# Making the weight sums of a seven-product last projection in another stage, partly by accumulating transfers

## The chip, the cores and the metric

The kernel runs on one core of one Trainium2 chip. The metric is device time in microseconds; the kernel before takes 1702.14 us, the median of three runs from 1701.0 to 1705.25. In the profile PE is TensorE's matmul, PEld its weight load, DVE is VectorE, ACT is ScalarE, POOL is GpSimd and SP is SyncE. SP, ACT and POOL also issue DMA transfers (SPq, ACTq, POOLq), each in its own program order.

## What is computed

The reference is a decoder trunk of two layers. Each layer mixes tokens in three branches and then adds a gated feed-forward with a causal convolution. A final norm ends it. The change touches only the feed-forward of the second layer and what feeds it:

```python
def conv_ffn(h, w_up, conv_w, conv_b, w_down):
    S = h.shape[1]
    u = h @ w_up                                   # 512 x 1024 @ 1024 x 5632
    up = jnp.pad(u, ((0, 0), (CONV_WIDTH - 1, 0), (0, 0)))
    c = conv_b
    for j in range(CONV_WIDTH):
        c = c + conv_w[j] * up[:, j:j + S]
    gate, val = jnp.split(c, 2, axis=-1)
    return (jax.nn.silu(gate) * val) @ w_down      # 512 x 2816 @ 2816 x 1024
...
    for l in range(DEPTH):
...
        x = x + conv_ffn(rmsnorm(x, norm2_g[l]), ffn_w_up[l], ffn_conv_w[l], ffn_conv_b[l], ffn_w_down[l])
    return rmsnorm(x, final_g)
```

## The kernel before

All tensors are float32. A product is made to float32 accuracy from three matmuls (`mm3`, L151): each operand is split into a rounded high part and a low remainder, and high by low, high by high and low by high are summed in PSUM. A weight tile of 128 by 512 (256 KB) is loaded by SP into `wr` (`load`, L121) and split by `part` (L131): ScalarE makes the high part (L139, `wh` or `sh`), VectorE the low one (L140, `wl` or `sl`). `unit` (L99) hands the splits out in the order of a plan that a first pass over the program writes down. It keeps splits a few tiles ahead of the matmuls (`AHEAD`: three in the up projection of a layer, four in the first part of the last projection) and loads three, or there six, tiles ahead of the splits. The framework's scheduler decides the final order of each engine's instructions from their priorities and dependencies. Where the code says `keep_in_program_order` (also as `po`), the order written is kept.

A layer's mixer is followed by the output projection (`wout`), by `ffn_up`, and then by `ffn_down` in layer 0 or by `last` in layer 1.

`ffn_up` makes 44 outputs of 128 by 512 (ff columns by tokens), in the order gate i, value i for i = 0 to 21. Each output is 8 k-tiles times 3 matmuls. VectorE takes it from PSUM (L1082, `fu`), ScalarE and VectorE apply the convolution (L1084 to L1086, `cv`), ScalarE the silu (L1090), and VectorE multiplies (L1091, `fth`). In layer 0 each `fth` is split for `ffn_down`. In layer 1 every second one goes with the one before it, a and b, to `halves` (L1100), which serves `last`. For odd i below 17 `ffn_up` of layer 1 also transposes a tile of x by way of DRAM on POOL's queue (`turned`, L227 to L230, `xT`, `tr` and `xt`).

`last` is the second layer's down projection, the residual and the final norm. It works on pairs of ff chunks, q = 0 to 10, as a product of 2 by 2 blocks by seven block products instead of eight. The weight blocks of pair q are w0 = W[2q] columns 0 to 511, w1 = W[2q] columns 512 to 1023, and w2, w3 the same of W[2q+1]. The activation blocks are the token halves a0, a1 of chunk 2q and b0, b1 of chunk 2q+1. The products 7, 5, 6 and 4 take sums of weight blocks and of activation halves, the products 1, 2 and 3 take w0, w2 and w3 as they are. `last` first runs the products 7, 5, 6, 4 over all q (the last pair in the order 6, 7, 5, 4), 6 matmuls for each weight tile, then product 1 over all q, then 2, then 3. All seven are in PSUM, and the output quarters are put together from them by VectorE (`addx`, `plus`, `post`) with factors of 0.5 or -0.5, the residual in `xt` and the squares for the norm.

The sums of the weight blocks do not depend on x. In the kernel before they are made during layer 0's `ffn_up` (q = 0 to 3) and `ffn_down` (q = 4 to 10), at the places in the table `PRE`. `presum` (L237) loads the four blocks of pair q with POOL's queue into `pre` tiles, and at its next call has VectorE make the four sums in place (L242 to L245) and POOL's queue store them to DRAM as `ts` tiles (L248). In `ffn_up` the tiles come from the 39 tiles of the pool `ff0`, in `ffn_down` from the pool `up`. `last` loads the sums from `ts` as it loads other weights, from the fifth tile on at most ten tiles ahead.

`halves` (L1100) makes for pair q the activation sums `s` and `d` in tiles named `wh` and `wl` by VectorE in operations of 256 columns, and a third sum in place over b's first half. It splits `s` and `b` (two splits of 512 columns: a ScalarE copy and a VectorE subtraction each). POOL's queue stores a0 and b0 as `ab` and d's first half as `s4`, which `last` loads and splits as it goes (`side`, `fetch`, `both`). The final gain `fg` is loaded on POOL's queue after the second pair of `last`.

In the span layer 0's `ffn_up` begins a few us before 511 and its `ffn_down` ends shortly before 866. The second `ffn_up` begins a few us before 1358 and ends at about 1586. `last` runs from there on, with its four summed products up to 1646.

Of the kernel before, what the change touches and what calls it, by code (L numbers as in the profile page):

```python
# [15 lines left out]
L = 2  # L16
# [3 lines left out]
NFF = 22  # L20
# [5 lines left out]
PRE = {(0, "f", 2): 0, (0, "f", 4): 1, (0, "f", 6): 2, (0, "f", 8): 3, (0, "d", 0): 4, (0, "d", 1): 5, (0, "d", 2): 6, (0, "d", 3): 7,  # L26
       (0, "d", 4): 8, (0, "d", 5): 9, (0, "d", 6): 10}
SEQ = "0 H 0 S 0 U S U S 0 S 0 0 S 2 2 Y 0 0 2 1 2 1 2 1 2 1 2 1 2 1 1 1"
NRAW = 3
AHEAD = {None: 2, "p": 4, "r": 3, "f": 3, "u": 5, "q": 4}  # L30
# [21 lines left out]
class Emit:  # L52
    def __init__(self, ctx, tc, a, plan=None):
# [5 lines left out]
        tp = lambda n, b, **k: ctx.enter_context(tc.tile_pool(name=n, bufs=b, **k))  # L59
        self.cp = tp("cp", 1)  # L60
# [60 lines left out]
    def load(self, u):  # L121
        name, l, i, c0, n, _ = u
        raw = self.u(n="wr") if u[5] == "q" and self.nraw % 2 else self.wp.tile([128, 512], F32, name=self.nm("wr"), tag="wr", bufs=NRAW)
        src = self.tsum[i] if name == "tsum" else self.a[name][l, i]
# [112 lines left out]
    def presum(self, l, stage, m):  # L237

        if self.pre:
            q, b = self.pre.pop()  # L240
            V = self.nc.vector
            V.tensor_tensor(b[3], b[3], b[1], op=SUB)  # L242
            V.tensor_tensor(b[1], b[1], b[0], op=SUB)
            V.tensor_tensor(b[0], b[0], b[3], op=ADD)
            V.tensor_tensor(b[2], b[2], b[0], op=SUB)  # L245
            for p, t in zip((7, 5, 6, 4), (b[3], b[1], b[0], b[2])):
                self.tsum[q, p] = self.dp.tile([128, 512], F32, name=self.nm("ts"))
                self.nc.gpsimd.dma_start(self.tsum[q, p], t)  # L248
        q = PRE.get((l, stage, m))
        if q is not None:  # L250
            b = self.fpre.pop(0) if stage == "f" else [self.u(n="pre") for _ in range(4)]
            for i, t in enumerate(b):
                self.nc.gpsimd.dma_start(t, self.a["wdt"][0, 2 * q + i // 2][:, i % 2 * 512:i % 2 * 512 + 512])
            self.pre.append((q, b))
# [69 lines left out]
    def run(self):  # L324
        nc, tc, a, V = self.nc, self.tc, self.a, self.nc.vector
        self.con = self.cp.tile([128, NCC], F32, name="con")
        self.pre, self.tsum = [], {}
# [730 lines left out]
    def ffn_up(self, l, st, x):  # L1058
# [10 lines left out]
        if l == 0:  # L1069
            self.fpre = [[self.f(n="pre") for _ in range(4)] for _ in range(4)]  # L1070
        for i in range(NFF):
            if l == 0 and i % 2 == 0 and 2 <= i <= 10:
                self.presum(l, "f", i)
# [5 lines left out]
            for j in (i, NFF + i):  # L1079
# [7 lines left out]
                cs.append(t)  # L1087
            g, v = cs
# [44 lines left out]
    def last(self, act):  # L1133
# [301 lines left out]
```

## Time and profile before

| | us |
|---|---|
| median of 3 runs | 1702.14 |
| lowest and highest run | 1701.0, 1705.25 |
| the profiled execution's own time | 1701.55 |
| its span | 1699.8 |
| TensorE busy | 1686.0 |
| VectorE busy | 1216.0 |
| ScalarE busy | 800.5 |
| GpSimd busy, DMA issues included | 240.7 |
| mean granted TensorE clock | 0.999 of full speed |

A page of the profile has numbered parts. Part 1 gives the busy time of each engine; a busy TensorE is not one at its peak, since matmuls overlap. The chain that ended last is followed back from the last instruction, at each step to what released it or to the instruction before it on its engine; its pieces in order of time read "start, length, what, how many". A window row gives, for one stretch of time, its length, the busy time of PE, PEld, DVE, ACT and POOL with the number of instructions, the granted clock, the share of the 16 DMA engines in use and the GB/s. A timeline row is "start, duration, engine, line, operation, output<-input, count", with the idle time just before it and what ended it in brackets. A row of a tile's instructions gives the shortest, median and longest duration in ns, then the first and last start.

### The profile page before, as it was taken

How to read it: one execution, taken by the hardware profiler on the slowest of the kernel's cores; microseconds unless marked ns; L12 is line 12 of the kernel's file. 1: busy time of each engine (PE TensorE's matmuls, PEld its weight loads, DVE VectorE, ACT ScalarE, POOL GpSimd, SP SyncE). 2: the span in 40 equal slices, each digit the busy share in tenths (PEclk: the TensorE clock that was granted, in tenths of full speed). 3: DMA queues.
4: the chain of work that ended last, by engine and by line, in shares of the span. 5: the costliest groups of instructions: out<-in, count | busy, mean ns of one | idle time of the engine just before them, and what ended most of it. 6: DMA issues, size and time to landing. Idle time of an engine off the chain costs nothing.

```text
span 1699.8 us, 27851 instructions
## 1 busy us (share of the span) xinstructions
PE 1686.0 (99%) x10214; PEld 1379.6 (81%) x10214; DVE 1216.0 (72%) x2113; ACT 800.5 (47%) x1367; POOL 240.7 (14%) x336
## 2 busy tenths in 40 slices
PE   9999999999999999999999999999999999999998
PEld 7888777788888888888888888778888888888886
DVE  6887746578669877655568888455786698887776
ACT  6563433453345444433346544335542554444565
POOL 2121000003301200003321210000132022110000
PEclk9999999999999999999999999999999999999999
DMA  5236553525544533147743265535254443443775
GB/s 182 87 109 203 174 180 94 174 93 164 190 148 143 196 120 99 63 144 261 247 150 98 91 205 181 179 101 185 88 165 158 155 133 127 134 134 112 242 242 166
DMA packets 147768, 260.01 MB, mean 153 GB/s; under 512 B 19600, under 2 KB 39952, under 8 KB 147632
## 3 DMA queue, kind: packets, MB, share of 16 engines
q1 hardware_dynamic: 122960, 192.87, 36.1%
q0 software_dynamic: 15888, 49.95, 8.9%
q10 hardware_dynamic: 8784, 15.42, 2.5%
q8 instruction: 80, 1.31, 0.3%
q14 instruction: 56, 0.46, 0.1%
HBM read 212.94 MB, written 45.22 MB: 152 GB/s over the span
## 4 chain that ended last, share of the span: by engine, by line
PE 85%; DVE 6%; DMA 5%; issue 2%; ACT 2%; SPq 1%; ACTq 0%; POOL 0%; DVEq 0%; POOLq 0%
PE acc L156 77%; PE sm L664 2%; PE sm L156 2%; DMA wr<-wall 2%; DVE wl L140 2%; PE sm L917 1%; PE sm L571 1%; DMA tr<-bkT 1%; DVE cs L790 1%; DMA wr<-wdt 1%; DVE TMP L788 1%; DMA bkS<-tr 1%; ACT wh L139 1%; DVE sl L140 1%; ACT sh L139 0%
## 5 line engine op out<-in xcount | busy, mean ns | idle before, releaser
L156 PE MATMUL acc<-lo,sh 128*128 128x512 f32 x1108 | 432.3, 391 | 0.2 <-ACT sh L139 0.2
L156 PE MATMUL acc<-hi,sh 128*128 128x512 f32 x1108 | 432.4, 390 | 0.0
L156 PE MATMUL acc<-hi,sl 128*128 128x512 f32 x1108 | 431.0, 390 | 0.2 <-DVE sl L140 0.2
L139 ACT CAST sh<-wr 128x512 fp32r<-128x512 f32 (+1 forms) x375 | 228.8, 616 | 368.6 <-PE acc L156 220.0
L140 DVE TENSOR_TENSOR sl<-wr,sh 128x512 fp32r<-128x512 f32 (+1 forms) x375 | 255.0, 684 | 108.8 <-ACT sh L139 79.3
L140 DVE TENSOR_TENSOR wl<-wr,wh 128x512 fp32r<-128x512 f32 x238 | 168.7, 712 | 144.7 <-ACT wh L139 141.3
L139 ACT CAST wh<-wr 128x512 fp32r<-128x512 f32 x238 | 146.8, 619 | 243.7 <-PE acc L156 139.3
L156 PEld LDWEIGHTS acc<-hi,sl 128*128 128x128 f32 x1108 | 208.1, 188 | 44.4 <-DVE sl L140 0.6
L156 PEld LDWEIGHTS acc<-lo,sh 128*128 128x128 f32 x1108 | 208.1, 188 | 44.3 <-issue 0.9
L156 PEld LDWEIGHTS acc<-hi,sh 128*128 128x128 f32 x1108 | 208.1, 188 | 42.9 <-issue 0.3
L156 PE MATMUL acc<-lo,wh 128*128 128x512 f32 x588 | 232.2, 395 | 1.3 <-ACT wh L139 0.8
L156 PE MATMUL acc<-hi,wl 128*128 128x512 f32 x588 | 230.4, 392 | 1.0 <-DVE wl L140 1.0
L156 PE MATMUL acc<-hi,wh 128*128 128x512 f32 x588 | 229.5, 390 | 0.0
L156 PEld LDWEIGHTS acc<-hi,wl 128*128 128x128 f32 x588 | 110.4, 188 | 26.7 <-DVE wl L140 3.0
L156 PEld LDWEIGHTS acc<-lo,wh 128*128 128x128 f32 x588 | 110.4, 188 | 26.4 <-ACT wh L139 1.6
L156 PEld LDWEIGHTS acc<-hi,wh 128*128 128x128 f32 x588 | 110.5, 188 | 22.1 <-issue 0.2
L156 PE MATMUL acc<-ah,sh 128*128 128x512 f32 x352 | 108.3, 390 | 0.0
L1084 ACT ACTIVATE cv<-fu,pc 128x512 f32<-128x512 f32 x88 | 71.6, 816 | 62.4 <-DVE fu L1082 62.3
L1082 DVE TENSOR_TENSOR fu<-acc,rsF 128x512 f32<-128x512 f32 x88 | 60.6, 688 | 39.1 <-PE acc L156 38.4
L1085 DVE SCALAR_TENSOR_TENSOR cv<-fu,pc,cv 128x511 f32<-128x511 f32 x88 | 65.9, 750 | 29.8 <-ACT cv L1084 29.8
L156 PE MATMUL acc<-wl,hi 128*128 128x512 f32 x212 | 86.2, 407 | 0.0
L156 PE MATMUL acc<-wh,hi 128*128 128x512 f32 x212 | 82.9, 391 | 0.0
(358 smaller groups left out, 2413.4 us busy)
## 6 DMA issues: line engine op xcount, KB each, us to landing
wr<-wall SPq DMA_DIRECT2D x488, 256.0 KB, 2.8
gd<-gth ACTq DMA_DIRECT2D x48, 256.0 KB, 3.2
gth<-gd POOLq DMA_DIRECT2D x48, 256.0 KB, 3.5
pre<-wdt POOLq DMA_DIRECT2D x44, 256.0 KB, 5.6
ts<-pre POOLq DMA_DIRECT2D x44, 256.0 KB, 2.8
wr<-ts SPq DMA_DIRECT2D x44, 256.0 KB, 4.0
wr<-wdn SPq DMA_DIRECT2D x40, 256.0 KB, 4.1
wr<-wdt SPq DMA_DIRECT2D x33, 256.0 KB, 3.7
```

The costliest lines, as they stand in the source:

```text
L139: self.kept(self.nc.scalar.copy(hi[:, :n], raw[:, :n]))
L140: self.kept(self.nc.vector.tensor_tensor(lo[:, :n], raw[:, :n], hi[:, :n], op=SUB))
L156: i = self.nc.tensor.matmul(*x, **y, **kw)
L571: i = T.matmul(pK[hv[1 - h], j, :], bk[hv[h], c, 1, :], x[hv[h], c, :], start=True, stop=True)
L664: po(T.matmul(o, l, r, start=start, stop=True, skip_group_check=True))
L788: V.tensor_tensor(tmp, NS[:, k + 1:, k:k + 1].to_broadcast([128, r, c]), TS[:, k:k + 1, :c].to_broadcast([128, r, c]), op=MUL)
L790: V.tensor_tensor(TS[:, k + 1:, :c], TS[:, k + 1:, :c], tmp, op=ADD)
L917: po(T.matmul(X[h][:, i, :], lhsT, rhs, start=new[h], stop=stop, skip_group_check=True))
L1082: V.tensor_tensor(u, ps, self.rsF, op=MUL)
L1084: A.activation(t, u, AF.Identity, scale=self.p("cw2", j), bias=self.p("cb", j))
L1085: V.scalar_tensor_tensor(t[:, 1:], u[:, :511], self.p("cw1", j), t[:, 1:], op0=MUL, op1=ADD)
```

## The change

The sums move from layer 0 to layer 1's `ffn_up` and the first pairs of `last`. They are made all positive: T7 = w1 + w3, T5 = w0 + w1, T6 = w0 + T7, T4 = w2 + T6. T7 and T5 are made by two transfers each, a load and then a load that adds to the tile (`accum_op`), cut into pieces of 128 elements (512 bytes). T6 and T4 are a load and one VectorE addition each. A generator, `sums`, spreads this over four calls for each pair; it is called once after each output of `ffn_up` (up to i = 20) and once after each of the first six pairs of `last`. Its `pre` tiles have a pool of their own, of six. The scratch space of the software descriptor ring is set to 4096 bytes a partition; the default, which the kernel before has, is 16384. Since the sums have other signs, `halves` makes other activation sums, and `last` subtracts in some places where it added.

In `halves` the two halves of the second split tile, `t`, now come from two different places, d's second half (a0 - a1) and b's second half (b1), and are split by separate instructions of 256 columns. Nothing is written over b any more.

```diff
-PRE = {(0, "f", 2): 0, (0, "f", 4): 1, (0, "f", 6): 2, (0, "f", 8): 3, (0, "d", 0): 4, (0, "d", 1): 5, (0, "d", 2): 6, (0, "d", 3): 7,
-       (0, "d", 4): 8, (0, "d", 5): 9, (0, "d", 6): 10}
+RING = 4096
...
+        self.pp = tp("pp", 6)
...
-        src = self.tsum[i] if name == "tsum" else self.a[name][l, i]
+        src = self.tsum[(l, *i)] if name == "tsum" else self.a[name][l, i]
...
-    def presum(self, l, stage, m):
-
-        if self.pre:
-            q, b = self.pre.pop()
-            V = self.nc.vector
-            V.tensor_tensor(b[3], b[3], b[1], op=SUB)
-            V.tensor_tensor(b[1], b[1], b[0], op=SUB)
-            V.tensor_tensor(b[0], b[0], b[3], op=ADD)
-            V.tensor_tensor(b[2], b[2], b[0], op=SUB)
-            for p, t in zip((7, 5, 6, 4), (b[3], b[1], b[0], b[2])):
-                self.tsum[q, p] = self.dp.tile([128, 512], F32, name=self.nm("ts"))
-                self.nc.gpsimd.dma_start(self.tsum[q, p], t)
-        q = PRE.get((l, stage, m))
-        if q is not None:
-            b = self.fpre.pop(0) if stage == "f" else [self.u(n="pre") for _ in range(4)]
-            for i, t in enumerate(b):
-                self.nc.gpsimd.dma_start(t, self.a["wdt"][0, 2 * q + i // 2][:, i % 2 * 512:i % 2 * 512 + 512])
-            self.pre.append((q, b))
+    def sums(self, l):
+
+        P, V, po, Q, T = self.nc.gpsimd, self.nc.vector, self.tc.keep_in_program_order, NFF // 2, {}
+
+        def get(q, p, n):
+            T[q, p] = self.pp.tile([128, 512], F32, name=self.nm("pre"), tag="pre")
+            add(q, p, n)
+
+        def add(q, p, n, **kw):
+            po(P.dma_start(T[q, p], self.a["wdt"][l - 1, 2 * q + n // 2][:, n % 2 * 512:n % 2 * 512 + 512], **kw))
+
+        def keep(q, *ps):
+            for p in ps:
+                self.tsum[l, q, p] = self.dp.tile([128, 512], F32, name=self.nm("ts"))
+                po(P.dma_start(self.tsum[l, q, p], T.pop((q, p))))
+
+        def both(q, o, i):
+            po(V.tensor_tensor(T[q, o], T[q, o], T[q, i], op=ADD))
+
+        for q in range(Q + 1):
+            if q:
+                both(q - 1, 6, 7)
+                keep(q - 1, 7, 5)
+            if q < Q:
+                get(q, 7, 1)
+                get(q, 5, 0)
+            yield
+            if q:
+                both(q - 1, 4, 6)
+                keep(q - 1, 6, 4)
+            yield
+            if q < Q:
+                add(q, 7, 3, accum_op=ADD, max_dma_last_dim=512)
+                add(q, 5, 1, accum_op=ADD, max_dma_last_dim=512)
+                get(q, 6, 0)
+                get(q, 4, 2)
+            yield
+            yield
+
+    def presum(self, l):
+        if l == L - 1:
+            next(self.sum, None)
...
-        if l == 0:
-            self.fpre = [[self.f(n="pre") for _ in range(4)] for _ in range(4)]
+        self.sum = self.sums(l)
         for i in range(NFF):
-            if l == 0 and i % 2 == 0 and 2 <= i <= 10:
-                self.presum(l, "f", i)
...
                 cs.append(t)
+                if i < 20 or i == 20 and j == i:
+                    self.presum(l)
...
-        V.tensor_tensor(s[:, h[0]], a[:, h[1]], b[:, h[1]], op=ADD)
-        V.tensor_tensor(s[:, h[1]], s[:, h[0]], a[:, h[0]], op=SUB)
-        V.tensor_tensor(d[:, h[0]], b[:, h[0]], s[:, h[1]], op=SUB)
+        V.tensor_tensor(s[:, h[0]], b[:, h[1]], a[:, h[1]], op=SUB)
+        V.tensor_tensor(d[:, h[1]], a[:, h[0]], a[:, h[1]], op=SUB)
+        V.scalar_tensor_tensor(s[:, h[1]], d[:, h[1]], -1.0, b[:, h[1]], op0=MUL, op1=SUB)
+        V.scalar_tensor_tensor(d[:, h[0]], s[:, h[1]], -1.0, b[:, h[0]], op0=MUL, op1=SUB)
         P.dma_start(self.s4[:, h[q % 2]], d[:, h[0]])
-        V.tensor_tensor(b[:, h[0]], a[:, h[0]], a[:, h[1]], op=SUB)
-        return self.split(s, at), self.split(b, at), ab, self.s4
+        t = hi, lo = at(), at()
+        for o, x in ((h[0], d[:, h[1]]), (h[1], b[:, h[1]])):
+            self.nc.scalar.copy(hi[:, o], x)
+            V.tensor_tensor(lo[:, o], x, hi[:, o], op=SUB)
+        return self.split(s, at), t, ab, self.s4
...
-            self.presum(l, "d", m)
...
-                return self.unit("tsum", 0, (q, p), 0)
+                return self.unit("tsum", L - 1, (q, p), 0)
...
+            if q < 6:
+                self.presum(L - 1)
...
-                v[2, q], v[3, q] = addx(pss[5][q], 1, 2 + q), addx(pss[5][q], 1, q)
+                v[2, q], v[3, q] = addx(pss[5][q], 1, 2 + q, -0.5), addx(pss[5][q], 1, q, -0.5)
...
-                V.tensor_tensor(y, y, f0[at - 1], op=ADD)
+                V.tensor_tensor(y, y, f0[at - 1], op=SUB if r else ADD)
...
-                plus(v[3, q], out[1][q], v[3, q])
+                plus(v[3, q], out[1][q], v[3, q], -0.5)
...
-            po(plus(y, out[3][r], y))
+            po(plus(y, out[3][r], y, -0.5))
...
-        nc = _bacc.Bacc("TRN2", target_bir_lowering=False, num_devices=1)
+        nc = _bacc.Bacc("TRN2", target_bir_lowering=False, num_devices=1, dynamic_dma_scratch_size=RING)
```

More of the change, by code (lines that the diff above doesn't have):

```diff
@@ L326, in run @@
         self.con = self.cp.tile([128, NCC], F32, name="con")
-        self.pre, self.tsum = [], {}
+        self.tsum = {}
         self.rst = self.cp.tile([128, 512], F32, name="rst")
@@ L1178, in half, with addx @@
             return t
-        def addx(ps, h, c):
+        def addx(ps, h, c, scale=0.5):
             y = self.r(n="v")
@@ L1185, in addx, with plus @@
                 x = self.xt[4 * h + j][:, c]
-                V.scalar_tensor_tensor(v(y), v(ps), 0.5, x, op0=MUL, op1=ADD)
+                V.scalar_tensor_tensor(v(y), v(ps), scale, x, op0=MUL, op1=ADD)
             return y
-        def plus(y, ps, z):
-            return V.scalar_tensor_tensor(y, ps, 0.5, z, op0=MUL, op1=ADD)
+        def plus(y, ps, z, scale=0.5):
+            return V.scalar_tensor_tensor(y, ps, scale, z, op0=MUL, op1=ADD)
         def square(y, s):
```

## The prediction

> **What bounds the kernel now.** I read the page from the top: busy time, then the chain that ended last, then windows over the stages.
>
> ```profile
> span 1699.8 us, 27851 instructions
> PE 1686.0 (99%) x10214; PEld 1379.6 (81%) x10214; DVE 1216.0 (72%) x2113; ACT 800.5 (47%) x1367; POOL 240.7 (14%) x336
> ```
>
> TensorE is without work for 13.8 us of 1699.8. A busy TensorE need not run at its peak, so the chain of waits gives the pace:
>
> ```profile
> 511.06 355.19 PE acc L156 x1567
> 1358.42 210.36 PE acc L156 x928
> ```
>
> 355.19 / 1567 and 210.36 / 928 are both 0.2267 us for one matmul, and nothing else stands between them. These are layer 0's up and down projections (where the old sums are made) and the second up projection (where the new ones go). The windows agree; columns are us, then busy us of PE, PEld, DVE, ACT, POOL, the clock, the DMA share and GB/s:
>
> ```profile
> 511.00:711.00 200.00, 200.00 (x884) 165.72 (x883) 159.80 (x243) 97.95 (x150) 15.03 (x28) 1.00 0.41 132
> 711.00:866.00 155.00, 155.00 (x685) 128.42 (x685) 87.53 (x140) 51.72 (x88) 34.33 (x64) 1.00 0.61 203
> 1358.40:1568.80 210.40, 210.40 (x930) 174.34 (x929) 173.57 (x280) 97.54 (x152) 35.10 (x64) 1.00 0.40 129
> 1568.80:1573.10 4.30, 3.94 (x16) 2.47 (x14) 4.30 (x8) 3.05 (x6) 0.54 (x1) 1.00 0.14 50
> 1594.00:1612.00 18.00, 18.00 (x80) 14.59 (x79) 13.36 (x22) 11.98 (x22) 0.00 (x0) 1.00 0.94 308
> 1692.60:1699.80 7.20, 0.00 (x0) 0.00 (x0) 1.90 (x5) 2.22 (x7) 0.00 (x0) 0.84 0.34 123
> ```
>
> The tail has 7.2 us of the 13.8, so 6.6 us are idle elsewhere, the start of the kernel included. The built program issues the same TensorE instructions in the same order, but for two neighbours that change places. So the change can win only stalls beside it, and it can lose whatever it makes TensorE wait for.
>
> **What it removes in layer 0.** 44 VectorE operations and 88 transfers of 256 KB on POOL's queue:
>
> ```profile
> L253 POOL DMA_DIRECT2D pre<-wdt x44: 536/538/543, 457.0 to 847.3; - x44
> L248 POOL DMA_DIRECT2D ts<-pre x44: 539/543/548, 539.4 to 857.1; - x44
> L242 DVE TENSOR_TENSOR pre<-pre,pre x11: 683/692/694, 538.4 to 854.0; 128x512 f32<-128x512 f32 x11
> ```
>
> That is 44 x 0.69 = 30 us of VectorE, 88 x 0.54 = 48 us of POOL and 23 MB. TensorE is busy 200.00 of 200.00 and 155.00 of 155.00 us there, so all of it lies behind matmuls: gain 0.
>
> **What it adds in the second up projection.** For each pair of ff chunks (q; 21.76 us, four outputs of 24 matmuls): two loads and two accumulating loads for the tiles 7 and 5, two loads for 6 and 4, two VectorE additions, four stores. Thus eight transfers, as in layer 0, and two VectorE operations in place of four. Layer 0 shows such a load beside an up projection:
>
> ```profile
> 538.00:559.80 21.80, 21.80 (x98) 18.07 (x97) 19.08 (x31) 10.18 (x17) 5.38 (x10) 1.00 0.61 212
> 1380.00:1401.80 21.80, 21.80 (x98) 18.06 (x97) 19.44 (x34) 11.15 (x19) 4.92 (x9) 1.00 0.42 143
> 1401.80:1423.50 21.70, 21.70 (x97) 18.01 (x96) 17.55 (x29) 9.46 (x16) 4.39 (x8) 1.00 0.41 132
> ```
>
> VectorE: 19 of the 22 additions stand before the last outputs, 19 x 0.69 = 13.1 us. The halves go from four operations of 256 columns and two of 512 to six and one. Two of these are of a form for which the nearest row of 256 columns is this:
>
> ```profile
> L1317 DVE SCALAR_TENSOR_TENSOR v<-v,frs,fg x2: 476/480/484, 1694.8 to 1695.2; 128x256 f32<-128x256 f32 x2
> 1567.31 0.42 DVE L1109 TENSOR_TENSOR wh<-fth,fth 128x256 f32<-128x256 f32 x1
> ```
>
> 4 x 0.42 + 2 x 0.48 + 0.69 = 3.33 us against 4 x 0.42 + 2 x 0.69 = 3.06, so 0.27 each, 2.7 in ten pairs. VectorE goes from 173.6 to 189.4 of 210.4 us, 90%; the window at 538 had 88% and the one at 1380 89%, both without a lost matmul. ScalarE gets one more operation per pair, at most 0.62 us, and stands at 46%. POOL gets eight issues of 0.54 us per pair, with the accumulating ones (four times the pieces) at 0.54 to 2.2 us: 4.3 to 7.6 us beside some 4 now, of 21.76. The smaller descriptor ring has no row; an overflow would show as longer POOL issues, and POOL has two thirds of its time to hide them. I cost all this at 0. If VectorE's cover were gone, TensorE would miss weight splits.
>
> The DMA share would go from 0.40 to about 0.7; at 0.61 in layer 0's down projection, with one such sum per 22 us, loads landed in 4.1 us and TensorE lost nothing.
>
> The signs in the last projection (subtractions, factors of -0.5) keep number and shape of the instructions: 0.
>
> **What the halves win.** Before, the last output of the up projection waits behind VectorE's queue:
>
> ```profile
> 1571.66 0.50 PE L156 MATMUL acc<-lo,sh 128*128 128x512 f32 x1 [0.17 <-ACT sh L139]
> 1573.12 0.50 PE L156 MATMUL acc<-hi,sl 128*128 128x512 f32 x1 [0.22 <-DVE sl L140]
> 1573.12 15.71 PE acc L156 x68
> 1591.56 2.76 PE acc L156 x12
> 1594.31 3.02 PE sm L156 x12
> 1594.59 0.42 DVE L1113 TENSOR_TENSOR fth<-fth 128x256 f32<-128x256 f32 x1 [0.81 <-DMA ab<-fth]
> ```
>
> 16 matmuls took 4.30 us where 16 x 0.2267 is 3.63, and the next 68 took 15.71 where 15.41 would do: 1.0 us. In the new VectorE order only six operations (3.2 us: 2 x 0.42, 2 x 0.48, 2 x 0.69) stand between the end of `fth` and that weight split, where nine (5.2 us) do now, so I take this 1.0 back whole. 3.02 against 2.72 is another 0.3, and the wait of 0.81 us for a transfer of `fth` goes, because `b` is no longer overwritten: 0.3 more. Sum: -1.3, with 0 as the other end.
>
> **What the last projection loses.** Here the sums are not free. The transfers of the last two pairs meet the stage that loads 256 KB every 1.36 us, at a DMA share of 0.94. These rows show how late its splits already are:
>
> ```profile
> 1600.53 0.62 ACT L139 CAST wh<-wr 128x512 fp32r<-128x512 f32 x1 [3.49 <-DMA wr<-ts]
> 1601.19 0.69 DVE L140 TENSOR_TENSOR wl<-wr,wh 128x512 fp32r<-128x512 f32 x1 [2.55 <-ACT wh L139]
> 1608.90 0.69 DVE L140 TENSOR_TENSOR wl<-wr,wh 128x512 fp32r<-128x512 f32 x1
> 1602.77 2.72 PE acc L156 x12
> 1613.65 2.72 PE acc L156 x12
> 1592.27 0.54 POOL L1112 DMA_DIRECT2D s<-wl  x1 [0.91 <-DVE wl L1111]
> 1592.81 1.08 POOL L1219 DMA_DIRECT2D fg<-fgr  x2
> ```
>
> The fourth pair's first split ends at 1601.88 and TensorE wants it at 1602.77: 0.9 us ahead, because its load was 3.49 us late. The sixth pair's ends at 1609.6, wanted at 1613.65: 4.1 us ahead. In POOL's new order, between the transfer at 1592.27 and the two `fg` stand two stores of pair 9, two accumulating loads and two loads of pair 10; after `fg`, four stores. The first six land before the sixth pair: 6 x 0.262 MB = 1.57 MB. At share 1 the window's 308 GB/s are 308 / 0.94 = 328 GB/s, so they take 4.8 us; the free 6% of 18 us is 1.1, the lead 0.9; TensorE waits 2.8. Ends: 0, if they go where loads have lead; and 7.1, if all but two stores land early and an accumulation counts twice (10 x 0.262 MB, 8.0 us, less 0.9). I take 2.8, as the two rows ahead say that loads are late there already. The last stores come some 11 us ahead of their loads, which went out up to here, so no wait:
>
> ```profile
> 1632.23 0.43 SPq L126 DMA_DIRECT2D wr<-ts  x1
> ```
>
> `fg` is 6 us later and first read at 1670. **Sum:** 0 - 1.3 + 2.8 = +1.5 on the profiled execution's 1701.55 us (span 1699.8 and 1.75 around it): 1703.0. The median, 1702.14, is 0.6 above that execution, so 1703.6.
>
> **The rivals.**
> A. Free transfers: the late stage has more lead than I count, and -1.3 stays: 1700.8. For it: VectorE stands earlier at the transition, so loads start up to 2.6 us sooner. Against it: the share of 0.94.
> B. Slower, the same place at its full price: 7.1 - 1.3 = +5.8, 1707.9, once the transfers delay the loads byte for byte. Its point is the fourth pair's 0.9 us of lead. The Trainium skill, "DMA: Bandwidth & Descriptors", section Queues, rings and completion order, has a rule for it: each DMA engine takes turns between queues packet by packet. By that rule POOL's burst takes half of the engines from the loads for as long as it lasts, and this rival's time is the better one; the 3.49 us beside two `fg` is in accord.
> C. Slower, accumulation: the trace has no accumulating transfer. VectorE's addition waits for it in order, with weight splits and evictions behind it, and TensorE behind these. From POOL's accumulating issue to that addition I count about 12 us (from the first output's half to two operations after the second's), and VectorE has some 2.6 us to spare per pair. An ordinary load takes this:
>
> ```profile
> DMA to landing us min/median/max: 2.3/4.4/7.6
> ```
>
> So it decides only from about 15 us, twice the longest. At 18 us each of ten pairs loses 3 us, less 8 us that the three splits ahead (3 x 2.72) cover: +22, 1724. Against it is that factor; for it, pieces of 512 bytes and twice the accesses.
> D. VectorE too full: 90% is the mean, and pairs with a transpose reach 97% (19.44 + 1.6 of 21.8). A lag of 1 us per pair is covered by those 8 us until the end, and then meets the late stage: +7, 1709. The windows at 538 and 1380 speak against it.
> E. It does not do what it says, i.e. layer 0 gives time back: excluded by 200.00 of 200.00.
>
> **How the numbers follow.** Forecast 0.45 (1703.6, its own range 1700.8 to 1707); A 0.12; B 0.23; C 0.14; D 0.06. 0.3%, about what a measurement here tells from no change, is 5.1 us, so the line is at 1707.2. Slower: three quarters of B, C, D, and a little of the forecast: 0.17 + 0.14 + 0.05 + 0.03 = 0.39. Faster needs 5.1 of the 6.6 idle us, most of which lie elsewhere: 0.03. Same: 0.58. The range runs from 1700.2 (A and some spread) to 1714, leaving out most of C.
>
> **What would show it.** Right: layer 0 unchanged; 928 matmuls in 210.4 us in the second up projection; no wait near 1571; one to three waits for weight splits around the third to fifth pair of the last projection, behind late `wr<-ts`, 1 to 5 us in all. Wrong: VectorE waiting for DMA before its additions (C); TensorE below its pace before 1568 (D); or a last projection at 0.2267 throughout (A).

## The result, and the profile after

| | before | changed |
|---|---|---|
| median, us | 1703.5 (1701.0 to 1705.63, 6 runs) | 1715.84 (1713.39 to 1717.07, 6 runs) |
| span of the profiled execution, us | 1699.8 | 1714.6 |
| TensorE busy, us | 1686.0 | 1692.2 |

The ratio is 1.0071, 95% interval 1.0061 to 1.0081: 12.3 us slower. The forecast was 1703.6 with a range to 1714.0, so the result lies outside it.

The head of the changed kernel's page, and two of its queue rows (packets, MB, share of 16 engines over the span):

```profile
span 1714.6 us, 27799 instructions
PE 1692.2 (99%) x10214; PEld 1381.1 (81%) x10214; DVE 1199.6 (70%) x2102; ACT 800.2 (47%) x1378; POOL 270.9 (16%) x358
...
q1 hardware_dynamic: 122960, 192.87, 36.1%
q0 software_dynamic: 27504, 55.72, 11.4%
```

TensorE's share is 99% as before; a page's averages do not show this loss. The chain that ended last does (start, length, what, how many):

```profile
511.84 355.19 PE acc L156 x1567
...
1361.11 90.45 PE acc L156 x399
1453.41 6.72 DMA wr<-wall
...
1479.31 5.65 DMA wr<-wall
1486.41 5.80 DMA wr<-wall
1506.53 3.89 DMA wr<-wall
1511.87 7.25 DMA wr<-wall
1530.51 69.05 PE acc L156 x296
1612.70 6.95 DMA wr<-ts
1619.71 11.68 DMA wr<-ts
```

Layer 0 is what it was: the same piece of 355.19 us for 1567 matmuls. The piece of 928 matmuls in the second up projection is broken after 399: between 1453 and 1530 loads of up-projection weights (`wr<-wall`) stand in the chain, where before there was nothing but matmuls. Two loads of sums (`wr<-ts`) follow in the last projection.

Windows of the changed kernel over the same stage (us; busy us of PE, PEld, DVE, ACT, POOL with counts; clock, DMA share, GB/s):

```profile
1361.10:1469.90 108.80, 108.80 (x482) 90.09 (x481) 87.53 (x148) 47.71 (x80) 48.52 (x76) 1.00 0.82 226
1469.90:1491.70 21.80, 19.23 (x78) 15.36 (x77) 19.62 (x34) 9.35 (x16) 11.47 (x18) 0.92 0.83 234
1491.70:1513.40 21.70, 20.16 (x87) 15.92 (x87) 17.67 (x32) 9.76 (x17) 11.42 (x18) 1.00 0.75 217
1513.40:1535.20 21.80, 19.05 (x76) 14.81 (x75) 16.47 (x29) 7.81 (x14) 10.28 (x18) 0.92 0.79 233
1535.20:1599.40 64.20, 64.20 (x285) 53.13 (x284) 55.15 (x92) 30.48 (x51) 22.22 (x36) 1.00 0.89 253
```

The loss is in 65 us of the stage: 241 matmuls take 65.3 us, where at 0.2267 us they take 54.6. The DMA engines are at 0.75 to 0.83 there, and at 0.82 and 0.89 in the stretches around it, in which TensorE loses nothing. So the share of the DMA engines by itself does not tell where time is lost.

Of the 10.7 us lost there, TensorE is idle for 6.86 (2.57, 1.54 and 2.75 in the three windows). Most of the rest is the granted clock, 0.92 in two of the windows. It is halved for 3.4 us each time, about 1.2 us after a stop of 2.57 us and after one of 2.03 us; after the stop of 1.54 us it is not:

```profile
1480.50:1483.90 3.40, 3.40 (x10) 2.63 (x9) 3.37 (x7) 0.07 (x1) 2.56 (x5) 0.50 0.85 245
1531.70:1535.10 3.40, 3.40 (x10) 2.65 (x9) 1.75 (x5) 0.62 (x1) 3.40 (x6) 0.50 0.83 237
```

Matmuls start 0.43 us apart in these 6.8 us, so about 3.2 of the 10.7 us are this (an estimate: 6.8 less 6.8 x 0.2267 / 0.43). So these two stops cost more than their own length.

To compare kernels by stage, I use two marks: the start of the long piece of the chain at the norm point of the second up projection (1358.42 before, 1361.11 after), and the first matmul of the last projection, the first that reads an `ah`. These rows are from the matmul timelines of the kernel before and the changed kernel:

```profile
1585.95 0.39 PE L156 MATMUL acc<-wl,ah 128*128 128x512 f32 x1
```

```profile
1599.38 0.39 PE L156 MATMUL acc<-wl,ah 128*128 128x512 f32 x1
```

The stretch from the one mark to the other takes 227.53 us before and 238.27 after; from the second mark to the end of the span it is 113.85 and 115.22. So the span's +14.8 is 2.7 ahead of the first mark, 10.7 in the second up projection, and 1.4 in the last one. The 2.7 is spread between executions: four experiments below (e5, e6, e7 and e13) have every TensorE instruction in the order of the changed kernel and start the stretch at 1357.66, 1359.24, 1360.34 and 1360.10.

What is waited for in the second up projection (1361 to 1586; us in total, times, longest), first before, then after, then the landing of the weight loads in each (1365 to 1565; count, size, median us):

```profile
ACT sh L139 <- DMA wr<-wall: 11.2, 4, 3.6
...
DVE sl L140 <- ACT sh L139: 0.8, 1, 0.8
```

```profile
ACT sh L139 <- DMA wr<-wall: 52.5, 22, 4.5
...
DVE sl L140 <- ACT sh L139: 20.4, 15, 3.5
...
PE acc L156 <- DVE sl L140: 6.1, 3, 2.6
...
DVE pre L254 <- DMA pre<-wdt: 0.6, 1, 0.6
```

```profile
wr<-wall SPq DMA_DIRECT2D x70, 256.0 KB, 2.6
```

```profile
wr<-wall SPq DMA_DIRECT2D x67, 256.0 KB, 4.6
```

ScalarE waits for loads, VectorE for ScalarE's copies, TensorE for VectorE's remainders. The first stop shows the order of events (a row of ScalarE, a window, a row of VectorE and one of TensorE):

```profile
1468.00 0.62 ACT L139 CAST sh<-wr 128x512 fp32r<-128x512 f32 x1 [4.17 <-DMA wr<-wall]
1469.40:1479.20 9.80, 7.36 (x33) 5.71 (x31) 9.63 (x18) 4.36 (x8) 4.53 (x9) 1.00 0.49 163
1478.60 1.28 DVE L140 TENSOR_TENSOR sl<-wr,sh 128x512 fp32r<-128x512 f32 x2
1479.34 0.50 PE L156 MATMUL acc<-hi,sl 128*128 128x512 f32 x1 [2.57 <-DVE sl L140]
```

A load is 4.17 us late. From then on VectorE works almost without a pause (9.63 of 9.80 us) on what has come together, and takes the remainder that TensorE waits for only at 1478.60. A late load and a full VectorE make the stop together.

The last row of the fence on the waits after is the sign that the prediction names for rival C, VectorE waiting for a transfer before an addition: 0.6 us, once. But the transfer is not an accumulating one. POOL stores the tiles 7 and 5 only when their accumulations have landed, and had done so before that addition; what VectorE still waited for was the plain load of tile 6, issued behind the two:

```profile
1401.66 1.07 POOL L251 DMA_DIRECT2D ts<-pre  x2
1402.67 0.69 DVE L254 TENSOR_TENSOR pre<-pre,pre 128x512 f32<-128x512 f32 x1 [0.57 <-DMA pre<-wdt]
```

The transition into the last projection, where the kernel before lost a us near 1571, lies in the last of the windows above, with 64.20 us busy of 64.20; e3 below tests the halves alone.

### The profile page after: what moved, and what is told of

The parts are those of the page before. It is cut to its first block, busy times and chain, and to the rows that moved or that the text cites. A ratio compares the mean times of both kernels' runs of the same rounds, so it can differ in the third digit from the quotient of the medians.

```text
span 1714.6 us, 27799 instructions
## 1 busy us (share of the span) xinstructions
PE 1692.2 (99%) x10214; PEld 1381.1 (81%) x10214; DVE 1199.6 (70%) x2102; ACT 800.2 (47%) x1378; POOL 270.9 (16%) x358
## 4 chain that ended last, share of the span: by engine, by line
PE 82%; DMA 7%; DVE 5%; issue 3%; ACT 2%; SPq 1%; POOL 0%; ACTq 0%; DVEq 0%; POOLq 0%
PE acc L156 74%; DMA wr<-wall 4%; PE sm L156 2%; PE sm L688 2%; DMA wr<-ts 1%; DVE wl L140 1%; PE sm L941 1%; DVE sl L140 1%; PE sm L595 1%; DMA tr<-qkt 1%; ACT sh L139 0%; ACT wh L139 0%; DMA tr<-bkT 0%; SPq L645 0%; PE sm L1046 0%
## 5 line engine op out<-in xcount | busy, mean ns | idle before, releaser
L156 PE MATMUL acc<-wh,lo 128*128 128x512 f32 x212 | 82.8, 390 | 0.0
```

Source lines behind the costliest of these rows:

```text
L156: i = self.nc.tensor.matmul(*x, **y, **kw)
```

## The experiments

The two marks, and what stands between them, for all runs. "Stretch" is first mark to second, "last" is second mark to the end of the span, "share" and "VectorE" are DMA share and busy us in 1361.2 to 1582.9, "landing" is the median of `wr<-wall` in 1365 to 1565. e1 to e4, e5 to e8 and e9 to e14 ran on three different chips; each ratio is to the kernel before on the same chip, whose median there was 1703.01, 1702.67 and 1702.72 to 1702.75 us.

| run | raw tiles | stretch | last | share | VectorE | landing | median time, us | ratio to before, 95% |
|---|---|---|---|---|---|---|---|---|
| before | 3 | 227.53 | 113.85 | 0.41 | 183.4 | 2.6 | 1703.5 | |
| changed | 3 | 238.27 | 115.22 | 0.84 | 182.5 | 4.6 | 1715.84 | 1.0061 to 1.0081 |
| e1 no accumulation | 3 | 226.60 | 116.58 | 0.68 | 192.7 | 3.6 | 1706.46 | 1.0010 to 1.0033 |
| e2 plain sums | 3 | 230.02 | 114.31 | 0.66 | 199.5 | 3.8 | 1705.65 | 1.0008 to 1.0028 |
| e3 halves only | 3 | 226.51 | 113.60 | 0.41 | 184.1 | 2.7 | 1701.88 | 0.9985 to 1.0002 |
| e4 before, small ring | 3 | 227.53 | 113.08 | 0.41 | 183.3 | 2.6 | 1702.19 | 0.9989 to 1.0010 |
| e5 overwrite, rows | 3 | 234.35 | 114.59 | 0.73 | 185.4 | 4.5 | 1708.83 | 1.0025 to 1.0052 |
| e6 overwrite, pieces | 3 | 232.41 | 115.65 | 0.74 | 186.9 | 4.4 | 1709.69 | 1.0024 to 1.0055 |
| e7 accumulate, rows | 3 | 239.35 | 117.61 | 0.77 | 182.0 | 4.7 | 1716.89 | 1.0066 to 1.0096 |
| e8 sums in layer 0 | 3 | 226.50 | 113.44 | 0.42 | 184.2 | 2.7 | 1700.96 | 0.9979 to 0.9998 |
| e9 changed, ring 2048 | 4 | 226.50 | 122.56 | 0.87 | 189.1 | 4.5 | 1708.78 | 1.0025 to 1.0049 |
| e10 plain sums | 4 | 226.50 | 112.52 | 0.67 | 204.1 | 4.0 | 1698.21 | 0.9964 to 0.9982 |
| e11 halves only | 5 | 226.66 | 113.51 | 0.42 | 185.6 | 2.6 | 1702.2 | 0.9991 to 1.0007 |
| e12 halves only | 4 | 226.50 | 112.86 | 0.42 | 185.1 | 2.6 | 1699.46 | 0.9973 to 0.9991 |
| e13 changed, ring 2048 | 3 | 231.70 | 118.70 | 0.85 | 187.9 | 4.1 | 1714.13 | 1.0052 to 1.0078 |
| e14 changed, ring 4096 | 4 | 226.51 | 114.90 | 0.86 | 192.5 | 4.7 | 1699.7 | 0.9974 to 0.9994 |

In e11 the chain's view does not reach back to the first mark, so it is taken from the matmul rows (1360.13). Where a stretch loses time, VectorE's busy time in the fixed window is lower because less of the work falls into it. In e5, e6, e7 and e13 the engines' instructions stay in the changed kernel's order. The scheduler ordered those of e1, e2, e9, e10 and e14 somewhat differently, and no run tells what that alone is worth.

### e1: the accumulating transfers left out

```diff
-                add(q, 7, 3, accum_op=ADD, max_dma_last_dim=512)
-                add(q, 5, 1, accum_op=ADD, max_dma_last_dim=512)
```

> The changed kernel with its two accumulating transfers per pair left out, so the tiles 7 and 5 (and 6 and 4 behind them) hold unfinished sums and the output differs; everything else stays. Theory 1 (the DMA engines of the second up projection are nearly full, weight loads land 4.6 us instead of 2.6 us after issue, TensorE waits for splits): the DMA share there falls from 0.65-0.92 to 0.60-0.70, the matmuls run at 0.227 us again, 7 us come back in that stage and some in the last projection: 1704 to 1708 us. Theory 2 (VectorE's work and its place cause the loss, the additions being in its way): nothing changes there, 1713 to 1717 us. Theory 3 (the ring of 4096 bytes): TensorE still loses where POOL's queue is dense: above 1710 us.

Measured 1706.46 us. Its chain has the whole stretch in one piece, and then the late stage:

```profile
1360.32 226.78 PE acc L156 x1000
1599.15 10.70 DMA wr<-ts
```

1000 matmuls in 226.78 us is the pace. 11.7 us of the stretch come back (238.27 to 226.60), which two transfers of eleven pairs had cost. ScalarE still waits 45.6 us in total for weight loads there, and TensorE loses nothing, so such waits by themselves cost nothing; they would from the point where the splits held ahead are used up.

### e2: all four sums by VectorE from plain loads, same place

```diff
+                both(q - 1, 7, 5)
+                both(q - 1, 5, 6)
                 both(q - 1, 6, 7)
...
-                get(q, 7, 1)
-                get(q, 5, 0)
+                get(q, 7, 3)
+                get(q, 5, 1)
...
-                add(q, 7, 3, accum_op=ADD, max_dma_last_dim=512)
-                add(q, 5, 1, accum_op=ADD, max_dma_last_dim=512)
```

> All four sums by VectorE from four plain loads, at the same place: eight transfers per pair in place of ten, four VectorE additions (0.69 us each) in place of two. Theory 1: as without accumulation, 1704 to 1709 us, DMA share 0.60-0.70 in the second up projection. Theory 2: VectorE gets 1.4 us more per 21.76 us, from 90% to 96%, and the time goes above the changed kernel's, 1717 us or more.

Measured 1705.65 us, as theory 1 has it: giving VectorE two more additions per pair is 10.2 us faster than the accumulation by the medians, 9.0 by the ratios to before. Theory 2 falls as a cause of the whole, but not entirely: beside e1, with the same eight transfers, the stretch is 3.4 us longer, and what was changed is VectorE's work. The window shows VectorE at 199.47 of 221.70 us:

```profile
1361.20:1582.90 221.70, 219.41 (x965) 180.26 (x964) 199.47 (x343) 102.01 (x172) 76.64 (x141) 1.00 0.66 217
```

### e3: the new halves alone

The new `halves`, with the signs in `last` that they need, and the old `presum` and `PRE`, with sums instead of differences:

```diff
-            V.tensor_tensor(b[3], b[3], b[1], op=SUB)
-            V.tensor_tensor(b[1], b[1], b[0], op=SUB)
+            V.tensor_tensor(b[3], b[3], b[1], op=ADD)
+            V.tensor_tensor(b[1], b[1], b[0], op=ADD)
             V.tensor_tensor(b[0], b[0], b[3], op=ADD)
-            V.tensor_tensor(b[2], b[2], b[0], op=SUB)
+            V.tensor_tensor(b[2], b[2], b[0], op=ADD)
```

> The kernel before with the new halves alone: the sums are made positive, but by VectorE in layer 0 at the old places, with the old ring. The prediction's term of -1.3 us for the halves: 1701.0 to 1703.0 us where the kernel before has 1702.5 to 1703.5, and no wait near the last output of the second up projection. Rival: the halves themselves cost (one more ScalarE copy, two slower VectorE forms): 1704 us or more.

Measured 1701.88 us, 1.1 below the 1703.01 of the kernel before on that chip; the interval of the ratio, 0.9985 to 1.0002, just holds 1. The trace has the mechanism: the piece that was broken at 1568.8 runs through into the last projection.

```profile
1358.99 226.68 PE acc L156 x1000
```

The stretch is 1.02 us shorter and the rest 0.25, together 1.27.

### e4: the small ring alone

```diff
-        nc = _bacc.Bacc("TRN2", target_bir_lowering=False, num_devices=1)
+        nc = _bacc.Bacc("TRN2", target_bir_lowering=False, num_devices=1, dynamic_dma_scratch_size=4096)
```

> The kernel before with a descriptor ring of 4096 bytes and nothing else. If the ring cost what the changed kernel loses ahead of its second up projection (2.7 us, 1.9 of it in the second layer's mixer): 1705 to 1706.5 us and POOL issues longer than 0.54 us. If not: within 0.5 us of the kernel before.

Measured 1702.19, ratio 0.9989 to 1.0010: the ring of 4096 bytes costs nothing here. The first mark, 1359.29, is 0.9 us later than in the kernel before, as e3's and e8's are by 0.6 and 0.9 us.

### e5, e6, e7: count of transfers, pieces, or the addition

e5 and e6 make the two accumulating transfers ordinary loads over the same tiles; e7 keeps the addition and drops the pieces. TensorE's, VectorE's, ScalarE's and SP's instructions stay in the changed kernel's order in all three.

```diff
-                add(q, 7, 3, accum_op=ADD, max_dma_last_dim=512)
-                add(q, 5, 1, accum_op=ADD, max_dma_last_dim=512)
+                add(q, 7, 3)                              # e5, and the same for 5
+                add(q, 7, 3, max_dma_last_dim=512)        # e6
+                add(q, 7, 3, accum_op=ADD, max_dma_last_dim=2048)   # e7
```

> The changed kernel with its two accumulating transfers per pair made ordinary loads of the same 256 KB over the same tiles, whole rows of 2 KB, so the sums are wrong and the output differs; ten transfers per pair as in the changed kernel, the order on every engine unchanged. If the count of transfers is what fills the DMA engines: share 0.84 again in the second up projection and 1713 to 1717 us. If the accumulation or its pieces are: two more rows' loads cost 2 x 128 x 92 ns = 24 us of 348 engine us per pair, share 0.68 + 0.07 = 0.75, 1706 to 1709 us.

> As the run before, but these ordinary loads are cut into 512-byte pieces as the accumulating ones are (the sums left out again). If a piece costs some 58 ns whether it adds or not: share 0.84, loads of weights landing at 4.6 us, 1713 to 1717 us. If the addition is what costs: share about 0.75, 1706 to 1709 us.

> The changed kernel with the accumulating transfers in whole rows of 2 KB, a quarter of the pieces, and the right sums. If the pieces cost: share 0.75 and 1706 to 1709 us, and POOL's accumulating issues fall from 1.3 to 0.54 us. If the addition itself costs, by byte: share 0.84 and 1713 to 1717 us, whatever POOL's issues take.

Measured 1708.83, 1709.69 and 1716.89 us. The packet rows (1365 to 1565) of e5, e6, e7 and the changed kernel, in this order:

```profile
q0 software_dynamic: 9368, 28.92, 44.5%
```

```profile
q0 software_dynamic: 9400, 29.03, 44.7%
```

```profile
q0 software_dynamic: 10168, 28.19, 49.0%
```

```profile
q0 software_dynamic: 16677, 28.81, 54.2%
```

e6 moved as many packets as e5: on plain loads the edit did not change what the DMA engines moved, so e6 is a second e5 and tells nothing of pieces. e7 and the changed kernel do: 10168 packets or 16677 for the same MB, and the same time. The pieces take DMA time (49.0% or 54.2%) but do not set the end. The addition does, though not alone (and e7, with the longest stretch, has a share of only 0.77): two more plain loads per pair cost 5.8 to 7.8 us of the stretch against e1 (232.41 and 234.35 against 226.60), and making them add costs another 3.9 to 6.9 (238.27 and 239.35).

An estimate of the price of one such 256 KB transfer, from these shares of 3200 engine us and the counts of `pre` and `ts` transfers in the same stretch, with e1's 39.1% as the base: about 13 engine us plain, 25 adding in rows, 35 adding in pieces. The packet records of the traces agree: a plain one is 64 packets of 4096 bytes at about 0.193 us (12.4 us), one adding in rows 128 packets of 2048 bytes at the same 0.193 us (24.8), one adding in pieces 512 packets of 512 bytes at about 0.066 us (33.7).

### e8: the same transfers in layer 0

```diff
-        if l == L - 1:
+        if l == 0:
             next(self.sum, None)
...
-        self.sum = self.sums(l)
+        if l == 0:
+            self.sum = self.sums(L - 1)
...
             xd.append(d)
+            if m < 6:
+                self.presum(l)
...
-            if q < 6:
-                self.presum(L - 1)
```

> The changed kernel's sums, accumulating transfers included, called after each output of layer 0's up projection (the last six calls in its down projection) and not in layer 1 and the last projection. Layer 0 has no transposes of x and no stores of halves there. Theory of full DMA engines: the share there goes to 0.75-0.80, TensorE loses 2 to 8 us there, the last projection loses nothing: 1703 to 1709 us. If it is the company of layer 1's other transfers on POOL's queue that makes the loss: no loss in layer 0, 1701 to 1703 us. Rival C of the prediction (VectorE waits for the accumulation): as in layer 1, 8 us or more.

Measured 1700.96 us. TensorE loses nothing beside the same accumulating transfers:

```profile
511.00:711.00 200.00, 200.00 (x884) 165.59 (x883) 160.84 (x245) 97.49 (x150) 57.40 (x82) 1.00 0.72 201
```

The theory of full engines expected a loss of 2 to 8 us at a share of 0.75 to 0.80, and there is none at 0.72. As the share stayed below what was expected, this alone is weak, and no loss is also what the company of layer 1's other transfers would give; e8 does not separate the two. What is also lower in layer 0 is VectorE's load, 80% of the window, and the landing of the weight loads, 3.5 us in 515 to 715. This and the 0.89 without loss in the changed kernel's own windows turned the theory from full engines to a loop: SP may load only into one of three tiles `wr`, and a tile is free again when ScalarE has copied it and VectorE has taken the remainder. The waits of SP's queue show it, before and after (1361 to 1586; us in total, times, longest): most loads go out when a subtraction ends.

```profile
SPq L126 <- DVE sl L140: 171.8, 72, 9.9
```

```profile
SPq L126 <- DVE sl L140: 162.7, 69, 10.0
```

At pace a tile is due every 2.72 us, so a tile has 3 x 2.72 = 8.16 us for its round. Before, the landing takes 2.6 of it, copy and subtraction 0.62 + 0.69, and 4.25 are left for waiting behind other work on ScalarE and VectorE. At a landing of 4.6 only 2.25 are left, and each wait beyond that makes the next load late as well. (The Trainium skill, "DMA: Bandwidth & Descriptors", section Queues, rings and completion order, has each DMA engine take turns between its queues packet by packet. The landings are in accord with it, though no run tests it: the loads have a queue of their own, `q1`, and their median goes from 2.6 us to between 3.6 and 4.7 with the other queue's traffic, not to twice.)

### e9, e13, e14: a fourth tile in the changed kernel

```diff
-NRAW = 3
-RING = 4096
+NRAW = 4                     # e9, e14; e13 keeps 3
+RING = 2048                  # e9, e13; e14 keeps 4096
...
-        self.pp = tp("pp", 6)
+        self.pp = tp("pp", 5)      # e14 alone
```

> The changed kernel with four tiles for weights just loaded in place of three, so that a load is issued one tile earlier (the ring goes to 2048 bytes to make room). Theory of the loop: with three tiles a tile has 3 x 2.72 = 8.16 us for the load, ScalarE's copy, VectorE's subtraction and the waits between; landing at 4.5 us and more with lag on VectorE overruns it. With four tiles it has 10.9 us: the second up projection goes from 238.3 us to 227-231, the whole to 1704-1709 us. Theory of the full engines (the DMA engines' time itself is the limit, share 0.84 and full for long stretches): one tile more only moves the queue, 236-239 us, 1713 us or more.

> The changed kernel with the ring of 2048 bytes and nothing else (three raw tiles), the order on every engine unchanged: the control of the run with four tiles. If that run's gain in the second up projection came from the fourth tile: 236 to 240 us here from the norm point to the last projection, and the whole 1715 us or more. If the small ring did it, by holding POOL's transfers back: near 227 us. If the ring is what cost that run 7 us in the last projection, POOL shows waits with no other releaser (issue) of several us here too, and the last projection is longer than 116 us.

> The changed kernel with four raw tiles and the ring of 4096 bytes; the room comes from five tiles for the sums in place of six. Loop theory: second up projection 226.5 to 228 us again. If the ring of 2048 bytes cost the earlier run its 7 us in the last projection: 114 to 117 us there and 1700.5 to 1704 us in all; if the accumulation itself did (VectorE's addition waiting for it, 8.1 us once): 120 us or more there and 1707 to 1710.

Measured 1708.78, 1714.13 and 1699.7 us. The stretch is 226.50 us in e9 and 226.51 in e14. The chain, the window and the landing of e14:

```profile
1355.89 226.68 PE acc L156 x1000
```

```profile
1361.20:1582.90 221.70, 221.70 (x980) 183.58 (x979) 192.46 (x326) 106.03 (x174) 101.73 (x160) 1.00 0.86 249
```

```profile
wr<-wall SPq DMA_DIRECT2D x70, 256.0 KB, 4.7
```

The DMA engines are busier than in the changed kernel (0.86), the loads land no sooner (4.7 us), all accumulating transfers are there, and TensorE is at 221.70 of 221.70. That decides between the theories: the loss was the loop's, not the engines'. That e14 has one tile fewer for the sums did not thin its traffic, as the share shows. With four tiles the round is 10.9 us, and 10.9 - 4.7 - 1.3 = 4.9 us are left, somewhat more than the 4.25 of the kernel before.

The runs with three tiles line up the same way. By the table's landings 3.25 us are left in e1, 3.05 in e2, 2.75 in e13, 2.45 in e6, 2.35 in e5, 2.25 in the changed kernel and 2.15 in e7; beside e3's 226.51 their stretches lose 0.1, 3.5, 5.2, 5.9, 7.8, 11.8 and 12.8 us. This is in accord with the loop, not a test of it, since the runs differ in more than the landing.

e9's gain in the stretch is in part the smaller ring's. The ring alone leaves 231.70 us there (e13), below the changed kernel's 238.27 and below the 236 to 240 expected, so this control was not neutral. The fourth tile is worth the other 5.2 us in e9, and 11.8 us in e14 at the ring of 4096 bytes. What the ring does is seen at the instructions of the tile `pre`, in e13 and then in e9 (1360 to 1640; POOL's idle us before them that no other work explains, times):

```profile
  issue: 54.3, 16
```

```profile
  issue: 60.4, 12
```

In the changed kernel it is 0.5 us. The ring of 2048 bytes holds POOL's queue back. A pair's two accumulating and two plain loads, which the changed kernel issues at one go (first row), come in two parts with as much as 9.75 us of idle POOL between them in e9 (the other rows):

```profile
1572.26 3.80 POOL L246 DMA_DIRECT2D pre<-wdt  x4 [0.22 <-issue]
```

```profile
1595.35 1.34 POOL L246 DMA_DIRECT2D pre<-wdt  x1
1606.43 2.42 POOL L246 DMA_DIRECT2D pre<-wdt  x3 [9.75 <-issue]
1608.34 1.05 POOL L251 DMA_DIRECT2D ts<-pre  x1
```

In e13's stretch the weight loads land in 4.1 us in place of 4.6, at the same share (0.85 and 0.84); that the broken-up bursts are the reason is not tested. And the last sums come later into the last projection, which is 118.70 us in e13 and 122.56 in e9. There VectorE stands still for long once (e9, its timeline):

```profile
1615.79 0.69 DVE L254 TENSOR_TENSOR pre<-pre,pre 128x512 f32<-128x512 f32 x1 [8.09 <-DMA pre<-wdt]
```

It is 8.09 us, with splits behind it, and TensorE stops for 5.35 us. This looks like rival C, but it is not an accumulation that VectorE waits for. POOL stores tile 7 at 1608.34 without a wait, so that accumulation had landed 7 us before. What was late is the plain load of tile 6, one of the three transfers issued from 1606.43 on, behind the 9.75 us. With the ring of 4096 bytes e14 has 114.90 us there, within 1.3 of e3's 113.60.

### e10: the plain sums with four tiles

The edit of e2 with that of e9.

> The four sums by VectorE from plain loads, in the second up projection, with four such tiles and the ring of 2048 bytes. Loop: its second up projection goes from 230.0 us to 226.5-227.5, the whole from 1705.65 to about 1702.5. If VectorE's 90% is what costs there: 229.5-230.5 us, 1705 to 1706.

Measured 1698.21 us, 4.3 below the expected 1702.5, 7.4 below e2 and faster than both kernels, ratio to before 0.9964 to 0.9982. The stretch is 226.50, with VectorE at 92%:

```profile
1361.20:1582.90 221.70, 221.70 (x980) 183.66 (x979) 204.10 (x348) 106.51 (x174) 76.97 (x142) 1.00 0.67 223
```

So e2's 3.5 us were the loop's too: a VectorE with 90% frees the tiles later, and that costs while there are three of them.

### e11, e12: more tiles with the sums in the old place

```diff
-NRAW = 3
+NRAW = 5                     # e11
+NRAW = 4                     # e12
```

Both with the ring of 4096 bytes, on top of e3.

> The new halves with the sums by VectorE at the old places, with five such tiles and the ring of 4096 bytes, which makes the room. Its second up projection has no stall left (226.5 us), so nothing there; the mixers and the last projection, whose chain names late weight loads, may gain: 1697 to 1701.5 us. If their loads are late because they are issued by need and not by room: 1701.5 to 1702.5 us.

> The new halves with the sums by VectorE at the old places in layer 0, four raw tiles, ring of 4096 bytes. If the fourth tile is what made the plain sums with four tiles 4.5 us faster than the kernel before: 1697 to 1699.5 us. If it was the emptied layer 0 or the new place of the sums: 1701.5 to 1702.5 us, as with five tiles.

Measured 1702.2 and 1699.46 us. With the fourth tile alone the median is 2.4 us below e3's, which ran on another chip; the intervals of the ratios overlap (0.9973 to 0.9991 beside 0.9985 to 1.0002), so this gain is not clear of the noise. With the fifth tile it is gone. Where these few us lie I did not find: the stretch has no stall in either, and e12's profiled span, 1698.6, is only 0.5 below e3's. What the rest of e10's lead over the kernel before (4.5 us on its chip) comes from stays open.

## Why the prediction was wrong

**The step that failed** is in the part on the second up projection: "I cost all this at 0." By the runs it is +11.8 us (238.27 against 226.51 in e3). Three things went into it.

First, the count: "Thus eight transfers, as in layer 0". It is ten, two of them loads that add. Without the two the stretch is 11.7 us shorter (e1), so the text's own list (two, two and two loads, four stores) held the answer.

Second, the cover was stretched past what it had covered. The window at 538 has eight such transfers, VectorE at 88% and no lost matmul, and e1 repeats that in the second up projection. For what lies beyond it the prediction leaned on another stage: "at 0.61 in layer 0's down projection ... loads landed in 4.1 us and TensorE lost nothing". VectorE is at 87.53 of 155 us there, 56% by the row that the prediction quotes, and at 173.57 of 210.40, 82%, in the second up projection. A late load is harmless where the tiles come free soon after it.

Third, what gives way was not costed: the lookahead of the loads. The rivals C and D count the three splits held ahead as 8 us of cover, but not the three tiles behind them, whose round a late landing lengthens. That loads run three tiles ahead was known, and 8.16 - 4.1 - 1.3 could have been worked out from the quoted rows.

The prediction also priced lost time by the length of a wait alone. In the changed kernel about 3.2 of the 10.7 us are the halved clock after two stops.

**The other steps.**

- TensorE's pace as the bound, and layer 0 at 0: right. The piece of 1567 matmuls is 355.19 us in both kernels.
- The halves at -1.3: right in the trace, -1.27 (e3), of which 1.02 lie in the stretch and 0.25 behind it. The text names 1.0, 0.3 and "0.3 more" and sums them to 1.3; the trace has the 0.3 once. The timed median has -1.1 with an interval that reaches 1.0002.
- The ring at 0: right at 4096 bytes, by e4 and by POOL's 0.5 us in the changed kernel. A ring of 2048 bytes, which the prediction is not about, does change the course (e13).
- The share "about 0.7": 0.84 measured, 0.66 to 0.68 for eight transfers (e1, e2). The term was right for the count it was made for.
- The late stage at +2.8: right in kind, the chain has `wr<-ts` at 1612.70 and 1619.71. In size, against e3's 113.60 us: +1.6 in the changed kernel, +3.0 in e1, +0.7 in e2.

**The rivals.** A falls with the loss. B named the late stage, at 7.1 us: it is 0.7 to 4.0 in runs with three tiles and the ring of 4096 bytes. C had a price of the right order (+22) for another mechanism, and its sign was seen, but its cause was not: the waits of VectorE before an addition that are shown here (0.57 us in the changed kernel, 8.09 in e9) ended with a plain load issued behind the accumulating ones. No load or store of `pre` took more than 13.5 us to land in the changed kernel, below the 15 from which C counts. D's sign, "TensorE below its pace before 1568", is what was seen. Its cause is half of it: VectorE's load matters (e2 against e1, 3.4 us), but 92% is free with four tiles (e10). The result lies between D's 1709 and C's 1724, and no rival had late loads and a full VectorE together.

## What to carry to other kernels

Before adding transfers beside a stream of weight loads, work out the round of one buffer: buffers times the pace of the consumer, less the landing under the new traffic, less the work that frees the buffer. What is left has to cover the waiting behind other work on those engines, and a stage where it did cover proves nothing for one whose engine is fuller. One more buffer took the changed kernel from 1715.84 us to 1699.7 (e14, which has one tile fewer for the sums), plain sums from 1715.84 to 1705.65 (e2). In the profiled executions 11.8 us of e14's gain lie in the stretch, as the loop has it; another 5.2 lie ahead of the first mark, and no run tells why.

## What the runs showed of the hardware that I had not expected

- An accumulating transfer of 256 KB takes about 25 engine us in whole rows and 35 in 512-byte pieces, where a plain one takes about 13 (estimates from e1, e5, e7 and the changed kernel). POOL's issues of `pre`, plain ones among them, take 1.32 us in the median and up to 1.90 beside the pieces, against 0.54 and 0.57 where all are plain rows (e5). They overlap: the four of a pair take 3.80 us together.
- Pieces asked for on a plain load did not change the number of packets (9400 in e6, 9368 in e5); on an accumulating one they did (16677 against 10168).
- A descriptor ring of 2048 bytes made POOL wait 54.3 us in 16 places (e13), one of 4096 bytes 0.5 us in the changed kernel and 2.8 in e14.
- The DMA engines of the core ran at a share of 0.86 for 222 us, with weight loads landing at 4.7 us, and TensorE lost nothing (e14).
- After stops of TensorE of 2.57 and 2.03 us the granted clock was 0.50 for 3.4 us, beginning about 1.2 us after the restart; after one of 1.54 us it was not (changed kernel). The length of a stop alone does not tell: after one of 2.04 us in e14's last projection the clock stayed at 1.00.
